# A gated DeltaNet layer on one core: TensorE's first stage in a written order of slots, and reciprocal square roots by GpSimd's power operation

## The chip, the cores and the metric

One core of a Trainium2 chip runs the whole kernel. The metric is the device time of one execution in microseconds (us), as the median of several executions. A profile is taken from one further execution. The engines are TensorE (PE; PEld is its weight load), VectorE (DVE), ScalarE (ACT), GpSimd (POOL) and SyncE (SP), whose queue issues all DMA transfers here.

## The reference

One layer of a streaming encoder, for 4096 prompt tokens and 32 sample tokens, with 1024 channels:

```python
h    = rmsnorm(x, ln_pre)
proj = h @ w_in            # B_a, C_a, X_a, Z_a | q, k, v | Z_g | a_dec, b_beta
y_a  = B_a * conv3(C_a * X_a) * silu(Z_a)                  # group A
q, k, v = silu(conv4(qkv));  q, k = l2norm(q), l2norm(k)   # group B, 4 heads of 128
S_t  = exp(g_t) (I - beta_t k_t k_t^T) S_{t-1} + beta_t k_t v_t^T
o_t  = q_t^T S_t / sqrt(128);  y_g = rmsnorm_head(o) * silu(Z_g)
y    = x + rmsnorm(concat(y_a, y_g) @ w_out, ln_post)
```

The recurrence is worked out in chunks. For a chunk, `a_mat` is the strictly lower part of `k k^T` with decay and beta, and `T = (I + a_mat)^-1`; with T the chunk's new values are a few matrix products with the state S, and S moves on to the next chunk.

## The kernel before

The prompt is cut into 16 blocks of 256 tokens (two chunks of 128), and the kernel has three stages. **Stage 1** (until about 1320 us) does group B, block by block. **Stage 2** does group A and **stage 3** the output projection. The change is in stage 1, and in the small function `rsqrt` that all stages call.

A block of stage 1 projects 16 channel tiles in pairs, in the order k, k, q, q, v, v, z, z (`steps`). One tile is 24 matmuls of 128x256 in fp16 (`proj`, L388 to L390: weights and activations are split in a high and a low half, 3 products for each of 8 slices). ScalarE and VectorE make the convolution and silu of each pair (`qkv_pair`). Beside that run, for the same block or the one before:

- `gates` and `decays`: decay and beta of the block's tokens (tiles `ggate`, `gcs`, `gB`).
- `stage1(b, c)`: for chunk c, 8 transposes (tile `gt`, L426) for the norms, and then 4 fp32 matmuls of 128x256 (tile `gq`, L442), from which VectorE writes M (L443: k k^T with decay) and `at`. Four DMAs bring M's diagonal 32x32 parts to DRAM (`lad`, L450).
- `subst(b)`, once for both chunks: DMAs load all 32 triangles into one tile `la` (L485); VectorE computes a scale `rl` (L488 to L490); GpSimd multiplies `la` by it (L495) and then solves the 32 triangular systems in 31 pairs of one multiply and one subtract (L499, L500), each resting on the one before; the result goes to DRAM (`ltd`, L503) and comes back in 8 DMAs as `Tc` (L510).
- `merge(b)`: from the inverses of the 32x32 parts in `Tc`, that of the whole 128x128 chunk (tile `m`, L546 to L560). It has five steps on TensorE, each after a copy of the one before. The first (below: M1) needs `Tc`.
- `rec_a(b, c)` and `rec_b(b, c)`: the recurrence and its output.
- `prep_a`: GpSimd, VectorE and 4 to 8 small matmuls prepare weights for stage 2 in the gaps of 13 of the blocks (tiles `xtw`, `hl`).

The main loop calls `finish(prevs, si)` for the block before: merge at step 0, then the recurrence; `stage1` stands at steps 4 and 5 of the block itself, one step earlier in the last two blocks (`LS`). That is the order in the code. The order on each engine's queue is decided by the Tile framework, which simulates the program and takes from each engine's ready instructions; it need not follow the code. An engine's queue runs strictly in the order so found.

`rsqrt(x, y, t)` is 11 small VectorE operations: an integer estimate and three Newton rounds (L114 to L119). It is called for the norms of x (`xss`, in `xprep`), of q and k (`r`, in `rnorms`), of each chunk's output (`so`, in `rec_b`: twice for a block), and in stage 3 (`oss`).

Of the kernel before, what the change touches and what calls it, by code (L numbers as in the profile page):

```python
# [10 lines left out]
BF16 = mybir.dt.bfloat16  # L11
# [23 lines left out]
LS = 2  # L35
# [15 lines left out]
def hybrid_kernel(  # L51
# [7 lines left out]
    V, G, A, T = nc.vector, nc.gpsimd, nc.scalar, nc.tensor  # L59
# [107 lines left out]

    def scaled(cts, n=P, urow=None):


        ws = []
        first = cts[0] >= 16
        nm = f"{cts[0]}"
        L = bank("r" if first else "g", [P, 2, P], f"L{nm}")[:, :len(cts), :n]
        for i, ct in enumerate(cts):
# [10 lines left out]
            if not first:  # L186
                for kn in (4, 2, 1):
                    V.tensor_tensor(ab[:, 0:kn], ab[:, 0:kn], ab[:, kn:2 * kn], ALU.add)
            for k in range(kn):
                T.matmul(L[:, i], ones16, ab[:, k, :], start=k == 0, stop=k == kn - 1)  # L190
            ws.append(w)
        e = te([P, 2, P], I32, "we", 1, nm)[:, :len(cts), :n]
# [8 lines left out]
        for i, w in enumerate(ws):  # L201
            V.tensor_tensor(w, w, bc(e[:, i].bitcast(F32), 1, KT), ALU.mult)
        if urow is None:
# [4 lines left out]
        return ws  # L208
# [13 lines left out]
    def xprep(b):  # L222
# [7 lines left out]
        ss = te([P, 3, 2], F32, "xss", 2, b["id"])[:m, :, :n // m]  # L230
# [12 lines left out]
        rsqrt(ss[:, 0], ss[:, 1], ss[:, 2])  # L243
# [138 lines left out]
    def proj(b, cts, nm):  # L382
        n = b["n"]
        pt = bank("pj", [P, 2, NB1], f"{b['id']}_{nm}")
        for i, ct in enumerate(cts):
            wh, wl = W[ct]
            for k in range(KT):
                T.matmul(pt[:, i, :n], wh[:, k, :], b["hi"][:, k, :n], start=k == 0, stop=False)  # L388
                T.matmul(pt[:, i, :n], wh[:, k, :], b["lo"][:, k, :n], start=False, stop=False)  # L389
                T.matmul(pt[:, i, :n], wl[:, k, :], b["hi"][:, k, :n], start=False, stop=k == KT - 1)  # L390
        return pt

    def qkv_pair(b, c0, dst):

        n = b["n"]
        pt = proj(b, (16 + c0, 17 + c0), f"c{c0}")
# [11 lines left out]
    def z_pair(b, c0):  # L408
        n = b["n"]
        pt = proj(b, (28 + c0, 29 + c0), f"z{c0}")  # L410
# [4 lines left out]
    def stage1(b, c):  # L415
# [4 lines left out]
        ss = b["ss"]  # L420
        nm = f"{b['id']}_{c}"
        jk = te([P, P], BF16, "jk", 2, nm)
        for x in range(2):
            tp = bank("g", [P, NH, P], f"t{x}{nm}")
            for h in range(NH):
                T.transpose(tp[:C, h, :], qk[:, h, x, sl], ident)  # L426
            for h in range(NH):
                A.activation(jk[:C], tp[:C, h, :], AF.Square, accum_out=ss[:, c, x, h:h + 1])
            if x == 0:
                kd = (te if b["s"] else tl)([P, NH, P], F32, "hl" if b["s"] else "kd", 4, nm)[:C]  # L430
                V.tensor_tensor(kd, tp[:C], bc(b["ed"][:, c], 2, P), ALU.mult)
                b["kd"].append(kd)
# [18 lines left out]

    def rnorms(b):
# [63 lines left out]
    def merge(b):  # L516
# [26 lines left out]
        for q in (0, 2):  # L543
# [3 lines left out]
            V.tensor_tensor(X[s1], px[s1], bc(nb_[s1], 3, 32), ALU.mult)  # L547
        for q in (0, 2):
# [16 lines left out]
    def rec_a(b, c):  # L565
# [4 lines left out]
        qk, v, U, kd = b["qk"], b["v"], b["U"][c], b["kd"][c]  # L570
        S = state[b["s"]]
# [21 lines left out]
        A.activation(vn, pv, AF.Copy)  # L593
        pS = bank("r", [P, NH, P], f"S{nm}")
# [6 lines left out]
        b["rec"] = (o, vn)  # L601

    def rec_b(b, c):
# [4 lines left out]
        o, vn = b["rec"]  # L608
# [4 lines left out]
        so = tl([P, 3, NH], F32, "so", 2, nm)[:C]  # L613
# [6 lines left out]
        rsqrt(so[:, 0], f, so[:, 2])  # L620
        V.tensor_tensor(f, f, b["cc"][:, c], ALU.mult)
        V.tensor_tensor(o, o, bc(f, 2, P), ALU.mult)
        pm = bank("o", [P, NH, P], f"m{nm}")[:, :, :C]
# [10 lines left out]
    def setup_block(b):  # L634
# [10 lines left out]
        b["kd"], b["M"], b["at"] = [], [], []  # L645

    def prep_b(ct):

        for i, w in enumerate(scaled((ct, ct + 1))):
# [6 lines left out]

    wa = {"next": 0}

    def prep_a():
# [7 lines left out]
        if not half:  # L667
            wa["w"] = scaled((ct, ct + 1))
# [70 lines left out]
    wgf, = scaled((32,), 8, ug)  # L739
# [8 lines left out]
    def finish(prevs, si):  # L748

        for p in prevs:  # L750
            n = p["nch"]
            if si == 0:
                merge(p)
            elif si == 1:
                rec_a(p, 0)
            elif si == 2:
                rec_b(p, 0)
                if n > 1:
                    rec_a(p, 1)
            elif si == 3:  # L760
                if n > 1:
                    rec_b(p, 1)
                if p["last"]:
                    out_state(p)

    prevs = []
    for gi, grp in enumerate(groups):
        for b in grp:
            setup_block(b)
            if b["s"]:  # L770
                b["hist"] = te([P, 12, 3], F32, "hists", 2, "i")
                if gi:
                    for c in range(0, 12, 2):
                        init_hist(b, 16 + c)
                state[1] = te([P, NH, P], F32, "hl", 4, "s0")
                dma(state[1], state_gdn[0, 0].rearrange("h k v -> k h v"))
            elif gi:
                b["hist"] = groups[gi - 1][-1]["hist_new"]
        for si, (kind, c0) in enumerate(steps):
            if gi == 0 and si == 4:  # L780
# [3 lines left out]
            if gi == 0:  # L784
                for kd_, c_ in steps[:si + 1 + (AH if si >= AS else 0)]:
                    ct = (28 if kd_ == "z" else 16) + c_
                    if ct not in W:
                        prep_b(ct)
                if kind != "z":
                    init_hist(smp, 16 + c0)  # L790
            for b in grp:
                n = b["n"]
                if kind == "z":
                    z_pair(b, c0)
                elif kind == "v":
                    qkv_pair(b, c0, b["v"][:, c0 - 8:c0 - 6, :n])
                else:
                    h0 = c0 % 4
# [454 lines left out]
```

## Time and profile before

| | |
|---|---|
| time, median of 3 (lowest to highest) | 2394.66 us (2390.61 to 2403.79) |
| the profiled execution: time, span | 2393.51 us, 2391.8 us |
| mean granted TensorE clock | 0.962 |
| busy: PE / PEld / DVE | 2156.4 / 1706.8 / 1699.0 us |
| busy: ACT / POOL | 992.5 / 1195.2 us |

The span runs from the first to the last instruction; the time is 1.7 us longer. PE is busy for 90% of the span, so it is near to being the bound as a whole. But a share over the whole span says nothing of one stage: in stage 1 a chain over all engines and four DMA legs runs beside the projections, and which of the two limits must be read from the waits there. The granted clock is the share of full speed that TensorE was allowed; 1 is 2.4 GHz, and 0.50 is 1.2 GHz.

### The profile page before, as it was taken

What the parts mean: (1) busy time and instruction counts of PE and PEld (TensorE: products, weight loads), DVE (VectorE), ACT (ScalarE), POOL (GpSimd) and SP (SyncE); (2) the same over time, 40 slices, a digit from 0 to 9 for tenths busy, and PEclk for the clock granted to TensorE, in tenths of its full rate; (3) what the DMA queues carried; (4) which work ended last, traced back from release to release, by engine and by line L of the source; (5) the groups of instructions that cost most, each with busy time, mean ns of one, the idle gap of its engine ahead of it and who ended that gap; (6) DMA issues with size and microseconds to landing.
All of it is one profiled execution on the core that took longest, in us unless ns stands there. A gap on an engine that the chain in (4) does not pass through costs nothing. (4 is left out here: it accounts for less than half of the span.)

```text
span 2391.8 us, 48652 instructions
## 1 busy us (share of the span) xinstructions
PE 2156.4 (90%) x18626; PEld 1706.8 (71%) x18626; DVE 1699.0 (71%) x4666; ACT 992.5 (41%) x2497; POOL 1195.2 (50%) x1581
## 2 busy tenths in 40 slices
PE   3677989899999999999999799899999999999998
PEld 3566877778777777787778678788888887444443
DVE  4886878987689888786777675676575565666763
ACT  4454656565666566555654220222121121433321
POOL 3526246752575644454454740766456611554542
PEclk9888999999999999999989899999999999999999
DMA  6334333534333442244324304311211133443431
GB/s 117 53 93 106 80 75 96 116 82 92 92 100 78 109 112 75 68 91 118 70 72 125 101 24 174 104 66 54 80 59 39 54 100 98 136 150 115 157 115 54
DMA packets 296913, 221.39 MB, mean 93 GB/s; under 512 B 166392, under 2 KB 236856, under 8 KB 296680
## 3 DMA queue, kind: packets, MB, share of 16 engines
q1 hardware_dynamic: 296680, 218.28, 33.5%
q8 instruction: 146, 2.39, 0.4%
q14 instruction: 87, 0.71, 0.1%
HBM read 127.84 MB, written 74.64 MB: 85 GB/s over the span
## 5 line engine op out<-in xcount | busy, mean ns | idle before, releaser
L388 PE MATMUL pj_c<-hhi,w 128*128 128x256 f16 x1536 | 429.3, 280 | 1.2 <-DMA hhi<-xth 1.2
L390 PE MATMUL pj_c<-hhi,w 128*128 128x256 f16 x1536 | 429.7, 280 | 0.0
L389 PE MATMUL pj_c<-hlo,w 128*128 128x256 f16 x1536 | 428.9, 279 | 0.0
L867 PEld LDWEIGHTS <-w_a 128*128 128x128 f16 x2880 | 269.9, 99 | 59.5 <-issue 25.6
L1130 PEld LDWEIGHTS <-opm 128*128 128x128 f16 x1536 | 149.6, 98 | 189.8 <-issue 15.5
L500 POOL TENSOR_TENSOR lt<-lt 128x112 f32<-128x112 f32 (+29 forms) x496 | 250.0, 504 | 38.9
L495 POOL TENSOR_TENSOR la<-la,lt 128x1024 f32<-128x1024 f32 x16 | 38.7, 2421 | 449.9 <-DVE lt L490 270.9
L390 PEld LDWEIGHTS <-w 128*128 128x128 f16 x2176 | 215.5, 100 | 53.2 <-POOL w L652 23.0
L499 POOL TENSOR_TENSOR lt<-la,lt 128x112 f32<-128x112 f32 (+29 forms) x496 | 233.1, 470 | 38.8
L388 PEld LDWEIGHTS <-w 128*128 128x128 f16 x2176 | 215.8, 100 | 34.1 <-issue 2.1
L389 PEld LDWEIGHTS <-w 128*128 128x128 f16 x2176 | 215.7, 100 | 30.7 <-issue 0.5
L405 DVE SCALAR_TENSOR_TENSOR qk<-u,cw,qk 128x256 f32<-128x256 f32 x384 | 214.9, 596 | 9.0 <-ACT qk L403 8.4
L867 PE MATMUL pja<-op,w_a 128*128 128x256 f16 x1536 | 194.5, 276 | 7.0 <-DVE w L881 3.4
L1079 POOL TENSOR_TENSOR mab<-mab 128x1024 bf16<-128x1024 bf16 (+2 forms) x48 | 103.6, 2159 | 130.8 <-ACT mab L1077 128.4
L867 PE MATMUL ga<-op,w_a 128*128 128x256 f16 x1152 | 149.8, 275 | 14.0 <-DVE w L881 8.1
L389 PE MATMUL pj_z<-hlo,w 128*128 128x256 f16 x512 | 144.6, 282 | 0.0
L390 PE MATMUL pj_z<-hhi,w 128*128 128x256 f16 x512 | 144.4, 282 | 0.0
L388 PE MATMUL pj_z<-hhi,w 128*128 128x256 f16 x512 | 144.3, 282 | 0.0
L1130 PE MATMUL pjo<-w_o,opm 128*128 128x512 f16 x528 | 118.2, 379 | 3.8 <-DVE v13y L1154 2.0
L1130 PE MATMUL ro<-w_o,opm 128*128 128x512 f16 x504 | 114.7, 383 | 3.9 <-DVE v7y L1154 2.0
L881 DVE TENSOR_TENSOR w<-pja,w 128x256 f32<-128x256 f32 x168 | 67.4, 420 | 70.6 <-PE pja L867 68.0
L1130 PE MATMUL go<-w_o,opm 128*128 128x512 f16 x504 | 112.7, 379 | 3.9 <-DVE v19y L1154 2.0
(707 smaller groups left out, 4946.5 us busy)
## 6 DMA issues: line engine op xcount, KB each, us to landing
xt<-in_x_prompt_dram SPq DMA_DIRECT2D x32, 512.0 KB
op<-hTd SPq DMA_DIRECT2D x32, 512.0 KB
mx<-mxd SPq DMA_DIRECT2D x16, 1024.0 KB
xtw<-in_w_in_dram SPq DMA_DIRECT2D x28, 512.0 KB
wad<-hl SPq DMA_DIRECT2D x56, 256.0 KB
gB<-gd SPq DMA_DIRECT2D x16, 516.0 KB
hTd<-hhi SPq DMA_DIRECT2D x16, 512.0 KB
hTd<-hlo SPq DMA_DIRECT2D x16, 512.0 KB
```

Of the source, the lines that this page charges most:

```text
L388: T.matmul(pt[:, i, :n], wh[:, k, :], b["hi"][:, k, :n], start=k == 0, stop=False)
L389: T.matmul(pt[:, i, :n], wh[:, k, :], b["lo"][:, k, :n], start=False, stop=False)
L390: T.matmul(pt[:, i, :n], wl[:, k, :], b["hi"][:, k, :n], start=False, stop=k == KT - 1)
L405: V.scalar_tensor_tensor(d, u[:, i, j:j + n], cw[:, j, c0 + i:c0 + i + 1], d, ALU.mult, ALU.add)
L495: E.tensor_tensor(la, la, bc(rl, 1, 32), ALU.mult)
L499: E.tensor_tensor(tm, bc(la[:, j, j + 1:32], 2, w), bc(lt[:, j, 0:w], 1, r), ALU.mult)
L500: last = E.tensor_tensor(lt[:, j + 1:32, 0:w], lt[:, j + 1:32, 0:w], tm, ALU.subtract)
L867: T.matmul(out, lt(x, k), rh(y, k), start=start and k == n == 0, stop=stop and k == 3 and n == 2)
L881: V.tensor_tensor(dst, p, src, ALU.add)
L1079: G.tensor_tensor(ab[:, 0:m], ab[:, 0:m], ab[:, m:2 * m], ALU.add)
L1130: T.matmul(p, mo[:, x, k, t * P:t * P + m], WO[y, k][:, hf * 512:hf * 512 + 512], start=k == i == 0, stop=k == KT - 1 and i == 2)
```

## The change

Four things, of which the diff shows the core:

1. Every TensorE instruction goes through a small class `Ordered`. While `T.on` is true (from block 1 to the end of stage 1) each is chained behind the one before, so that PE's queue is exactly the order of the code.
2. The code of blocks 1 to 15 is written in slots. A block has 16 slots, one after each channel tile, and a function cut into parts by `yield` runs its parts in numbered slots. M1 of block g stands in slot 8 of block g+1 (`s0 + 24`), the other merge steps in slots 9 to 12, the two `gram` (the `gq` matmuls and M) in slots 11 and 12, the transposes for the norms of k in 7 and 8 and of q in 10 and 11, `gates` in 9, 10 and 13. Blocks of stage 1 no longer differ at the end (`LS` is gone).
3. `rsqrt(x, y)` is one GpSimd operation, `pow` with an operand of -0.5.
4. `prep_a` is called after channel tile 7, waits for the previous block's `subst_end` alone, and its matmuls (now 2 instead of 8, after one more VectorE addition) stand in slots 11 and 13.

```diff
+    class Ordered:
+        on = False
+        last = None
+        def queue(self, i):
+            ins = getattr(i, "ins", i)
+            if self.on and self.last is not None:
+                tc.add_manual_dep(ins, self.last.name, mybir.DependencyInfo(
+                    mybir.DependencyClass.NoSync, mybir.DependencyReason.DATA), reason="order")
+            self.last = ins
+            return i
...
-    def rsqrt(x, y, t):
-
-        V.tensor_scalar(t.bitcast(I32), x.bitcast(I32), 1, None, ALU.logical_shift_right)
-        V.tensor_scalar(y.bitcast(I32), t.bitcast(I32), -1, float(0x5F3759DF), ALU.mult, ALU.add)
-        for _ in range(3):
-            V.tensor_tensor(t, y, y, ALU.mult)
-            V.scalar_tensor_tensor(t, t, -0.5, x, ALU.mult, ALU.mult)
-            V.scalar_tensor_tensor(y, t, 1.5, y, ALU.add, ALU.mult)
+    mhalf = const([P, 16], F32, "mhalf")
+    V.memset(mhalf, -0.5)
+
+    def rsqrt(x, y):
+
+        G.tensor_tensor(y, x, mhalf[:x.shape[0], :x.shape[-1]], ALU.pow)
...
+    def finish(p, s0):
...
+        at_slot(s0 + 22, next, ra[0])
+        at_slot(s0 + 23, next, ra[0])
+        for i in range(5):
+            at_slot(s0 + 24 + i, next, mg, None)
+        at_slot(s0 + 29, next, ra[0])
+        at_slot(s0 + 30, ends, ra[0])
+        at_slot(s0 + 30, next, rb[0])
+        at_slot(s0 + 28, next, ra[1])
+        at_slot(s0 + 32, next, ra[1])
+        at_slot(s0 + 34, next, ra[1])
+        at_slot(s0 + 34, ends, rb[0])
+        at_slot(s0 + 35, ends, ra[1])
+        at_slot(s0 + 35, next, rb[1])
+        at_slot(s0 + 39, ends, rb[1])
...
-            s1 = 4 if gi + LS < len(groups) else 3
-            if si in (s1, s1 + 1):
...
+            at_slot(s0 + 7, norm_qk, b, 0, 0)
+            at_slot(s0 + 8, norm_qk, b, 1, 0)
+            at_slot(s0 + 10, norm_qk, b, 0, 1)
+            at_slot(s0 + 11, gram, b, 0)
+            at_slot(s0 + 11, norm_qk, b, 1, 1)
+            at_slot(s0 + 12, gram, b, 1)
+            at_slot(s0 + 12, rnorms, b)
+            at_slot(s0 + 12, subst, b)
+            if gi + 1 < len(groups):
+                nx = groups[gi + 1][0]
+                g = gates(nx)
+                at_slot(s0 + 2, xprep, nx)
+                at_slot(s0 + 9, next, g)
+                at_slot(s0 + 10, next, g)
+                at_slot(s0 + 13, ends, g)
+            finish(b, s0)
+            for si, (kind, c0) in enumerate(steps):
+                ps = pair(b, kind, c0)
+                next(ps)
+                run_slot(s0 + 2 * si)
+                ends(ps)
+                run_slot(s0 + 2 * si + 1)
```

What it moves on the engines, at three places.

On TensorE before, M1 of one block (tile `m`, from `Tc` and `M`) stands inside a z tile (`w_30`) of the next one, a matmul at a time, and the `gq` of that next block begins between them:

```order
L388 MATMUL pj_z_15005<-hhi_13353,w_30_1926 128x256
L546 MATMUL m_14092<-Tc_13862,M_0_13648 32x32
L389 LDWEIGHTS w_30_1926
L389 MATMUL pj_z_15005<-hlo_13354,w_30_1926 128x256
L546 MATMUL m_14092<-Tc_13862,M_0_13648 32x32
L442 MATMUL gq_0_14702<-qk_14019 128x256 x2
L546 MATMUL m_14092<-Tc_13862,M_0_13648 32x32
L390 LDWEIGHTS w_30_1927
L390 MATMUL pj_z_15005<-hhi_13353,w_30_1927 128x256
```

M1 and the next block's `gq` stand side by side there, in the fifteenth of the block's 16 channel tiles.

On TensorE after, M1 is one piece behind the ninth tile (`w_24`, slot 8):

```order
L74 MATMUL pj_c_16834<-hhi_15618,w_24_1191 128x256
L74 MATMUL m_16864<-Tc_16303,M_0_16129 32x32 x4
L74 MATMUL m_16864<-Tc_16303,M_1_16199 32x32 x4
L74 MATMUL m_16864<-Tc_16303,M_0_16129 32x32 x4
L74 MATMUL m_16864<-Tc_16303,M_1_16199 32x32 x4
L77 MATMUL gt_1_16884<-ident,qk_16473 128x128 x4
L74 LDWEIGHTS w_25_1194
L74 MATMUL pj_c_16834<-hhi_15618,w_25_1194 128x256
```

It moved from the fifteenth tile to behind the ninth, and needs all 8 parts of `Tc` at once, where before the first needed one.

Further on in the same block, the second `gram` behind the thirteenth tile (`w_28`, slot 12):

```order
L74 MATMUL pj_z_17066<-hhi_15618,w_28_1487 128x256
L74 MATMUL m_16864<-U,Rx_16863 64x64 x8
L77 MATMUL rt_1_17100<-ident,v_15493 128x128 x4
L74 MATMUL gq_1_17112<-qk_16473 128x256 x2
L74 MATMUL gq_1_17117<-qk_16473 128x256 x2
L74 LDWEIGHTS w_29_1490
```

All of the merge and four channel tiles now stand between M1 and the `gq` of the next block.

On GpSimd before, `subst` runs through without anything between (`hl` in front is a weight of `prep_a`):

```order
L675 TENSOR_TENSOR hl_6_7578<-xtw_6500,hl_6_7578 128x512
L495 TENSOR_TENSOR la_8463<-la_8463,lt_8464 128x1024
L499 TENSOR_TENSOR lt_8464<-la_8463,lt_8464 128x31
L500 TENSOR_TENSOR lt_8464<-lt_8464 128x31
L499 TENSOR_TENSOR lt_8464<-la_8463,lt_8464 128x60
```

And after (L137 is the power operation; a third one, of the other chunk's `so`, stands further down among the pairs):

```order
L137 TENSOR_TENSOR r_13209<-ss_12458,mhalf 128x16
L544 TENSOR_TENSOR la_13218<-la_13218,lt_13219 128x1024
L548 TENSOR_TENSOR lt_13219<-la_13218,lt_13219 128x31
...
L548 TENSOR_TENSOR lt_13219<-la_13218,lt_13219 128x112
L137 TENSOR_TENSOR so_0_13417<-so_0_13417,mhalf 128x4
L549 TENSOR_TENSOR lt_13219<-lt_13219 128x28x4
L548 TENSOR_TENSOR lt_13219<-la_13218,lt_13219 128x135
L549 TENSOR_TENSOR lt_13219<-lt_13219 128x27x5
L548 TENSOR_TENSOR lt_13219<-la_13218,lt_13219 128x156
L137 TENSOR_TENSOR xss_13595<-xss_13595,mhalf 128x2
```

The powers came into GpSimd's queue in front of and inside the chain of the solve.

## Rows read from the trace of the kernel before

**Rows 1.** Busy times over twelve blocks: all engines; then PE on `m`, `gq`, `gt`, `ggate`.
```profile
core 0: us, PE busy (x) PEld busy (x) DVE busy (x) ACT busy (x) POOL busy (x), PEclk, DMA share, GB/s
331.20:1248.60 917.40, 850.74 (x7949) 721.04 (x7947) 744.12 (x2272) 535.60 (x1434) 501.89 (x904) 0.96 0.38 92
331.20:1248.60 917.40, 86.96 (x1286) 0.96 0.38 92
331.20:1248.60 917.40, 53.23 (x192) 0.96 0.38 92
331.20:1248.60 917.40, 33.76 (x192) 0.96 0.38 92
331.20:1248.60 917.40, 12.51 (x384) 0.96 0.38 92
```

**Rows 2.** Waits of PE, 200 to 1370 us: total us, times, longest.
```profile
PE m L546 <- DMA Tc<-ltd: 25.4, 17, 3.0
```

**Rows 3.** VectorE's timeline (start us, us) and summary of M, L443.
```profile
269.50 0.42 DVE L443 TENSOR_TENSOR M<-gq,gB 128x256 f32<-128x256 f32 x1
566.49 0.42 DVE L443 TENSOR_TENSOR M<-gq,gB 128x256 f32<-128x256 f32 x1
858.76 0.42 DVE L443 TENSOR_TENSOR M<-gq,gB 128x256 f32<-128x256 f32 x1
1173.67 0.42 DVE L443 TENSOR_TENSOR M<-gq,gB 128x256 f32<-128x256 f32 x1
L443 DVE TENSOR_TENSOR M<-gq,gB x64: 404/424/426, 161.7 to 1310.2; 128x256 f32<-128x256 f32 x64
```

**Rows 4.** PE's timeline: two projections, M1 of three blocks.
```profile
619.37 0.27 PE L388 MATMUL pj_z<-hhi,w 128*128 128x256 f16 x1
619.48 0.27 PE L389 MATMUL pj_z<-hlo,w 128*128 128x256 f16 x1
622.38 0.24 PE L546 MATMUL m<-Tc,M 32*32 32x32 f32 x2 [2.41 <-DMA Tc<-ltd]
630.33 0.69 PE L546 MATMUL m<-Tc,M 32*32 32x32 f32 x16
1370.91 0.31 PE L546 MATMUL m<-Tc,M 32*32 32x32 f32 x2 [6.09 <-DMA Tc<-ltd]
```

**Rows 5.** GpSimd's timeline: first and last operations of `subst` in three blocks.
```profile
580.92 2.48 POOL L495 TENSOR_TENSOR la<-la,lt 128x1024 f32<-128x1024 f32 x1 [46.28 <-DVE lt L490]
868.69 2.36 POOL L495 TENSOR_TENSOR la<-la,lt 128x1024 f32<-128x1024 f32 x1 [23.74 <-DVE xss L115]
907.34 0.20 POOL L500 TENSOR_TENSOR lt<-lt 128x8 f32<-128x8 f32 x1
1187.60 2.47 POOL L495 TENSOR_TENSOR la<-la,lt 128x1024 f32<-128x1024 f32 x1 [27.57 <-DVE lt L490]
1221.02 0.20 POOL L500 TENSOR_TENSOR lt<-lt 128x8 f32<-128x8 f32 x1
```

**Rows 6.** VectorE's timeline: the first and the last `rl` of one block.
```profile
575.91 0.19 DVE L488 TENSOR_SCALAR lt<-la 128x32 f32<-128x32 f32 x1
580.60 0.19 DVE L490 TENSOR_TENSOR lt<-lt,bl 128x32 f32<-128x32 f32 x1
```

**Rows 7.** SyncE's timeline: the way back of one block's solve.
```profile
618.67 0.34 SPq L503 DMA_DIRECT2D ltd<-lt  x1
620.39 4.29 SPq L510 DMA_DIRECT2D Tc<-ltd  x8
```

**Rows 8.** GpSimd's operations by shape: busy us, mean ns; then idle before.
```profile
L499 POOL TENSOR_TENSOR lt<-la,lt 128x16 f32<-128x16 f32 x16 | 4.3, 271 | 1.3
```

**Rows 9.** Two stretches around PE's longest gap (columns as in rows 1).
```profile
226.00:233.70 7.70, 0.42 (x5) 0.13 (x3) 3.57 (x9) 2.35 (x9) 5.58 (x20) 0.70 0.04 2
233.70:239.00 5.30, 5.30 (x25) 3.99 (x26) 0.00 (x0) 1.47 (x8) 0.74 (x5) 0.50 0.37 42
```

**Rows 10.** Summary of a line of `rsqrt`: duration ns min/median/max.
```profile
L117 DVE TENSOR_TENSOR so<-so x96: 99/163/1109, 292.6 to 1436.7; 128x4 f32<-128x4 f32 x96
```

More of the change, by code (lines that the diff above doesn't have):

```diff
@@ L34 @@
 SG = 0
-LS = 2
 XPE = 256
@@ L186, in scaled @@
             if not first:
-                for kn in (4, 2, 1):
-                    V.tensor_tensor(ab[:, 0:kn], ab[:, 0:kn], ab[:, kn:2 * kn], ALU.add)
-            for k in range(kn):
+                ab2 = e[:, i, 0:P // 2].bitcast(BF16)
+                for kn, o in ((4, ab[:, 0:4]), (2, ab[:, 0:2]), (1, ab2.unsqueeze(1))):
+                    V.tensor_tensor(o, ab[:, 0:kn], ab[:, kn:2 * kn], ALU.add)
+                sums.append(ab2)
+            for k in range(kn if first else 0):
                 T.matmul(L[:, i], ones16, ab[:, k, :], start=k == 0, stop=k == kn - 1)
             ws.append(w)
-        e = te([P, 2, P], I32, "we", 1, nm)[:, :len(cts), :n]
+        if not first:
+            yield
+            L = bank("g", [P, 2, P], f"L{nm}")
+            for i in range(2):
+                T.matmul(L[:, i], ones16, sums[i], start=True, stop=True)
         V.tensor_scalar(e.bitcast(F32), L, 2.0 ** -100, None, ALU.max)
@@ L202, in scaled @@
             V.tensor_tensor(w, w, bc(e[:, i].bitcast(F32), 1, KT), ALU.mult)
+        if not first:
+            yield
         if urow is None:
@@ L450, in stage1 @@
             dma(b["lad"][c, :, q].rearrange("h j i -> j h i"), M[s, :, s])
+    def stage1(b, c):
+        norm_qk(b, c, 0)
+        norm_qk(b, c, 1)
+        gram(b, c)
     def rnorms(b):
@@ L555, in merge @@
         A.activation(Y[0:64], pt, AF.Copy)
+        yield
         for c, h in ch:
@@ L667, in prep_a @@
         if not half:
-            wa["w"] = scaled((ct, ct + 1))
+            yield from scaled((ct, ct + 1))
             return
@@ L746, in hybrid_kernel, with at_slot, run_slot, ends @@
     steps = [("k", 4), ("k", 6), ("q", 0), ("q", 2), ("v", 8), ("v", 10), ("z", 0), ("z", 2)]
[L748 to L767, printed above, removed]
+    slots = {}
+    def at_slot(i, fn, *a):
+        slots.setdefault(i, []).append(lambda: fn(*a))
+    def run_slot(i):
+        for fn in slots.pop(i, ()):
+            fn()
+    def ends(gen):
+        for _ in gen:
+            pass
+    def finish(p, s0):
+        n = p["nch"]
+        ra = [rec_a(p, c) for c in range(n)]
+        rb = [rec_b(p, c) for c in range(n)]
+        mg = merge(p)
+        if n == 1:
+            for i, g in enumerate((ra[0], ra[0], mg, ra[0], ra[0], rb[0])):
+                at_slot(s0 + 16 + i, next, g, None)
+            at_slot(s0 + 24, ends, rb[0])
+            at_slot(s0 + 24, out_state, p)
+            return
+        at_slot(s0 + 22, next, ra[0])
[12 more added lines that the diff above has]
+        at_slot(s0 + 39, ends, rb[1])
+        if p["last"]:
+            at_slot(s0 + 36, out_state, p)
+    def first_group(grp):
         for b in grp:
@@ L826, in hybrid_kernel @@
         prevs = grp
-    while wa["next"] < 16:
-        prep_a()
+    T.on = False
     early.close()
-    for si in range(4):
-        finish(prevs, si)
+    for i in sorted(slots):
+        run_slot(i)
     late.close()
```

190 lines of the change are left out of this document (109 added, 81 removed).

## The prediction

> **What bounds the kernel now.** The page gives PE 90% of the span, so I first looked at whether stage 1 is bound by PE's work or by something that PE waits for. Over twelve blocks PE is busy for 850.74 of 917.40 us [rows 1]: 70.9 us of work for a block, and 5.6 us of idle time. The times at which a block's M is written come every 75.35 us: (1173.67 + 0.42 - 269.50 - 0.42) / 12 [rows 3]. So PE is close to the bound, and not quite there.
>
> The waits of PE then show what it is idle for: most of all `Tc`, 25.4 us in 17 waits, 3.0 at the longest [rows 2]. So there is a second bound that lies just as close, and it is a loop. A block's M goes through the DMAs and GpSimd's solve and comes back as `Tc` (I call this the chain); with `Tc` PE does M1 and some more work up to the next block's `gq`, from which the next M is written (the PE part). The period can't be shorter than chain plus PE part, whatever is in PE's queue elsewhere.
>
> The chain is read part by part, each from the rows of one block:
> - From M to GpSimd's first multiply: 858.76 + 0.42 to 868.69, which is 9.5 us; in another block 566.49 + 0.42 to 580.92, which is 14.0 [rows 3, 5]. In the latter the three small `rl` operations lay 4.7 us apart, 575.91 to 580.60, with other VectorE work between them [rows 6].
> - The solve: 1187.60 to 1221.02 + 0.20 is 33.6 us, 868.69 to 907.34 + 0.20 is 38.9 [rows 5].
> - The way back: `ltd` is issued at 618.67, the first `Tc` at 620.39, the eighth 4.29 us later [rows 7]; M1's first matmul ran at 622.38 [rows 4], 2.0 us behind the first issue. It needed the first part alone.
>
> So the chain to the first matmul of M1 lasts about 9.5 + 33.6 + 3.7 = 46.8 to 14.0 + 38.9 + 3.7 = 56.6 us, and with 75.35 as period some 19 to 28 us are left for the PE part. That part is short because M1 and `gq` stand side by side in PE's queue.
>
> **The change part by part.**
>
> *The slots.* After the change M1 stands behind tile 8 and the last `gq` behind tile 12. The PE part becomes a fixed list:
> - four channel tiles, 4 x 24 matmuls at 0.11 us (619.37 to 619.48, [rows 4]): 10.6
> - the merge: 8 of its 56 matmuls in one piece took 0.69 us [rows 4], which gives 4.8; in the loop as it is they take 86.96 / 12 = 7.2 [rows 1]. I take 5.5, nearer to the former, since they stand in pieces now.
> - both `gq`: 53.23 / 12 = 4.4; three quarters of the transposes `gt`: 33.76 / 12 x 3/4 = 2.1; `ggate`: 12.51 / 12 = 1.0 [rows 1]; the four transposes `rt` like `gt`: 4 x 0.176 = 0.7
> - M behind the last `gq`: 0.6, one operation of 0.42 [rows 3] and the way to it.
>
> That is 24.9 us. The chain now ends with the eighth `Tc`, since M1 is one piece: 1.7 us to the first issue, 4.3 for all eight, some 1.5 to land, 7.5 in all [rows 4, 7]. For its head I take 9.5, because VectorE gets relief (below) and the `rl` stand together; 14.0 is the other end. For the solve I take the middle, 36.2.
>
> PE has work for 70.9 - 24.9 = 46 us between the last `gq` and M1. The chain, worked out next, takes longer than that, so PE will stand before M1 in every block, with the z, k and q tiles that could fill the time locked behind it in the queue.
>
> *The powers.* One `rsqrt` on VectorE was 11 operations of about 0.163 us [rows 10], so 1.8 us; four in a block give back 7.2 us of VectorE. VectorE is busy for 744.12 of 917.40 us [rows 1], it isn't the bound, and the relief is worth only what it brings to the chain's head. On GpSimd, one power (`r`) lies ahead of the first multiply, in time in which GpSimd waits for `la` anyway; three stand inside the solve, and the solve is the path. No row shows a power. The lower bound is a multiply of nearly its size, 0.27 us for 128x16 [rows 8]; the upper one the multiply of 128x1024, 2.4 us [rows 5]. I take 0.8, between them in ratio, because it is a costlier function on a tiny tile: 3 x 0.8 = 2.4 us on the path. Their inputs come from the block before and the next `xprep`; if one is late, the solve waits for it.
>
> The Trainium skill, GPSIMD Engine Reference, section "4.1 Engine selection", speaks against the move: elementwise work on a tile belongs to VectorE, and GpSimd is about 2 times slower with two inputs. By that a power would be an estimated 2 x 0.163 = 0.33 us, and the sum 14 x 3 x 0.47 = 20 us lower, 2479; no row here shows a power.
>
> *The clock.* The only gap as long as the one I expect is at 226.00 to 233.70, where PE worked for 0.42 us; behind it PE ran for 5.30 us at a granted clock of 0.50, the level of 1.2 GHz [rows 9]. That loses 2.65 us, in the PE part, each time. The durations I used hold the mean clock 0.96 [rows 1], which is 1.0 us of 24.9; so 1.7 more.
>
> The Trainium skill, TensorE: Matmul & The Clock Gate, section "HAM oscillation — how this bites in real kernels", describes just that, bursts of matmuls between waits for data that each start at the lower clock. The row agrees; without the effect the sum would be 14 x 1.7 = 24 us lower, 2475.
>
> *The rest.* Chaining PE's instructions costs no time by itself, they ran in order already. `prep_a` gives up 6 small matmuls and takes a VectorE addition, off the path. The end of the last two blocks, where `LS` moved the `gram` forward, loses that: these two periods took 1310.2 + 0.42 - 1174.09 = 136.5 us together [rows 3].
>
> **The sum.** Chain 9.5 + 36.2 + 2.4 + 7.5 = 55.6. Period 55.6 + 24.9 + 1.7 = 82.2 us. Twelve periods: 12 x (82.2 - 75.35) = +82. The last two: 164.4 - 136.5 = +28. I leave the first block and stages 2 and 3 as they are, less the 6.09 us for which PE stood at the last M1 [rows 4], of which I take 5 back. In all +105 us on the profiled execution's 2393.51, which is 1.15 below the median: **2499 us**.
>
> **The rivals.**
> - *The chain at its shortest.* Solve 33.6, powers at 0.27, no loss of clock: 9.5 + 33.6 + 0.8 + 7.5 + 24.9 = 76.3. Then 12 x 0.95 + (152.6 - 136.5) - 5 = +22, 2416 us. For it: VectorE and GpSimd disturb each other less. Against: the long solve of 38.9 is as well attested as the short one.
> - *`Tc` comes before slot 8* (other side). If the chain falls below 70.9 - 24.9 = 46 us, PE never waits and the period is PE's work, 70.9: 12 x -4.45 + (141.8 - 136.5) - 5 = -53, 2340 us. The kernel becomes faster at all if the period falls below (12 x 75.35 + 136.5 + 5) / 14 = 74.7, so a chain under 49.8. For it: the VectorE relief, and PE's 5.6 us of idle time in small waits that a fixed order may remove. Against: the shortest parts that any of these rows shows, with the cheapest power, make 51.4.
> - *Dear powers.* At 2.4 us each, or with waits for their inputs that stop the solve for as long: 3 x 1.6 = 4.8 more a period, 14 x 4.8 = +67, 2566 us. For it: nothing else in these rows has as many inputs that come from elsewhere in the middle of the solve. Against: the tiles have 2 and 4 columns.
>
> **How the numbers follow.** The loop as summed 0.60, with a range of its own of 2435 to 2565 (the head at 9.5 to 14.0, the solve at 33.6 to 38.9, the merge at 4.8 to 7.2, not all at one end); the short chain 0.14; dear powers 0.12; `Tc` in time 0.14. The predicted time is the first's. From 2400 to 2580 all but the last case and the ends of the others lie inside, about 0.8. A measurement of this kernel can't tell less than 0.5%, 12 us, from no change. The fourth case gives faster 0.12 and 0.02 near no change; the second 0.04 near no change; all else is slower, 0.82.
>
> **What would show it.** Right: a wait of PE for `Tc` at M1 of about 10 us in each of 14 blocks, with the clock at 0.50 behind it; M every 82 us; M1 to the next M 25 to 28 us; chain 53 to 58 us; L137 rows on GpSimd under 1 us. Wrong: no wait at M1 (the fourth case), M every 76 us or less, power rows of 2 us, or a solve with gaps ahead of its powers. It would also be wrong if the solve itself became much shorter once VectorE does less beside it: that is the one large term that I carry over from before without a reason of its own.

## The result and the profile after

The changed kernel takes 2571.06 us (2564.86 to 2576.26, 4 runs) against 2394.26 us: a ratio of 1.073, with a 95% interval of 1.069 to 1.077. The profiled execution took 2564.86 us, 171 us more than that of before; the sums below are made against it.

The page's busy line and its row of TensorE's granted clock in 40 slices:

```profile
PE 2202.4 (86%) x18626; PEld 1755.8 (69%) x18626; DVE 1526.9 (60%) x3732; ACT 1003.2 (39%) x2497; POOL 1303.6 (51%) x1666
PEclk9878988888898889889988988999999999999999
```

VectorE lost 172 us of work and GpSimd gained 108. PE is busy for 46 us more, partly because its clock is lower. So most of the time went into waiting; the lower clocks are in the first 24 of the 40 slices, which are stage 1. M's rows on VectorE give the period, as in [rows 3]:

```profile
273.31 0.42 DVE L488 TENSOR_TENSOR M<-gq,gB 128x256 f32<-128x256 f32 x1
1334.99 0.42 DVE L488 TENSOR_TENSOR M<-gq,gB 128x256 f32<-128x256 f32 x1
L488 DVE TENSOR_TENSOR M<-gq,gB x64: 414/424/426, 160.8 to 1500.3; 128x256 f32<-128x256 f32 x64
```

Twelve periods took 1061.7 us, 88.5 each, against 75.35. The 171 us are made up of +3.8 up to the first of these rows, 12 x 13.1 = +157.5, +28.8 in the last two periods (1500.72 - 1335.41 = 165.3, before 136.5), and -18.8 from the last M to the end (2563.1 - 1500.7, before 2391.8 - 1310.6).

Over twelve blocks (columns as in [rows 1]), and what PE waited for there (as in [rows 2]):

```profile
369.50:1431.30 1061.80, 882.72 (x7905) 759.41 (x7903) 633.93 (x1725) 543.22 (x1436) 541.24 (x942) 0.89 0.33 77
```

```profile
PE m L74 <- DMA Tc<-ltd: 81.6, 108, 6.5
PE om L77 <- DVE o L679: 37.7, 7, 12.4
PE oo L74 <- DVE zg L685: 32.8, 13, 3.5
PE m L74 <- DVE Rx L596: 29.8, 14, 2.3
```

PE is idle for 14.9 us of a block (1061.80 - 882.72, over 12) and not 5.6, and the mean clock fell from 0.96 to 0.89. The largest wait is the one forecast, for `Tc` at M1: 81.6 us over the 14 blocks of this window, 5.8 a block, where the prediction expected about 10. Three others, at `om`, `oo` and in M1's second half, were not in the sum.

One M1 on PE's timeline shows both kinds. The eight parts of `Tc` come 0.55 us apart; then the second half waits for VectorE's product of the first:

```profile
1301.23 0.31 PE L74 MATMUL m<-Tc,M 32*32 32x32 f32 x2 [3.63 <-DMA Tc<-ltd]
1301.83 0.31 PE L74 MATMUL m<-Tc,M 32*32 32x32 f32 x2 [0.29 <-DMA Tc<-ltd]
...
1305.11 0.31 PE L74 MATMUL m<-Tc,M 32*32 32x32 f32 x2 [0.23 <-DMA Tc<-ltd]
1307.44 1.05 PE L74 MATMUL m<-Tc,M 32*32 32x32 f32 x16 [2.01 <-DVE Rx L596]
```

The clock in this block, ahead of M1, in it, and from there to the next M:

```profile
1250.90:1299.70 48.80, 44.40 (x388) 39.73 (x385) 32.90 (x80) 26.46 (x70) 35.42 (x68) 0.97 0.43 104
1299.70:1313.40 13.70, 8.46 (x56) 6.08 (x57) 3.28 (x7) 3.88 (x12) 11.19 (x15) 0.51 0.45 119
1313.40:1335.40 22.00, 21.14 (x216) 17.31 (x215) 11.59 (x46) 14.33 (x37) 2.91 (x1) 0.92 0.06 16
```

GpSimd's powers by shape, and two of one solve on its timeline:

```profile
L137 POOL TENSOR_TENSOR r<-ss,mhalf 128x16 f32<-128x16 f32 x16 | 46.6, 2913 | 353.4 <-DVE ss L507 353.4
L137 POOL TENSOR_TENSOR so<-so,mhalf 128x4 f32<-128x4 f32 x32 | 32.5, 1016 | 60.0 <-DVE so L676 30.2 <-DVE hist L429 27.3 <-ACT o L642 1.2
L137 POOL TENSOR_TENSOR xss<-xss,mhalf 128x2 f32<-128x2 f32 x16 | 11.2, 701 | 10.4 <-DVE xss L271 10.4
```

```profile
462.97 1.01 POOL L137 TENSOR_TENSOR so<-so,mhalf 128x4 f32<-128x4 f32 x1 [0.83 <-DVE so L676]
500.26 1.01 POOL L137 TENSOR_TENSOR so<-so,mhalf 128x4 f32<-128x4 f32 x1 [12.40 <-DVE hist L429]
```

The three powers inside the solve take 2 x 1.02 + 0.70 = 2.7 us. The second one of this solve held it up for 12.4 us more, since its input was not there. That is the longest such wait: GpSimd's idle time ahead of its powers is 0.8 to 13.2 us in each of the twelve solves of the table below, 4.2 in the mean.

The input was late because of `prep_a`, the fourth part of the change. VectorE makes the input (`so`, L676), and ahead of it in VectorE's queue stood the first operation on a weight of `prep_a`, which waited for the DMA of that weight:

```profile
497.74 1.23 DVE L204 TENSOR_TENSOR xtw<-xtw,lnp 128x1024 f32<-128x1024 f32 x1 [10.17 <-DMA xtw<-in_w_in_dram]
499.95 0.16 DVE L676 TENSOR_SCALAR so<-so 128x4 f32<-128x4 f32 x1
```

In the kernel before, the same operation never waited. Its group in stage 1, before and after; behind the second bar is VectorE's idle time ahead of it:

```profile
L182 DVE TENSOR_TENSOR xtw<-xtw,lnp 128x1024 f32<-128x1024 f32 x16 | 19.0, 1218 | 0.0
L204 DVE TENSOR_TENSOR xtw<-xtw,lnp 128x1024 f32<-128x1024 f32 x14 | 18.4, 1316 | 54.2 <-DMA xtw<-in_w_in_dram 54.2
```

In seven of the twelve solves the second power waits behind such a stop, for 37.0 of the 49.9 us that all powers wait there. PE's seven waits at `om` follow these seven stops, each some 5 us later.

### The profile page after: what moved, and what is told of

The parts are those of the page before. It is cut to its first block, busy times and chain, and to the rows that moved or that the text cites. A ratio compares the mean times of both kernels' runs of the same rounds, so it can differ in the third digit from the quotient of the medians.

```text
span 2563.1 us, 47756 instructions
## 1 busy us (share of the span) xinstructions
PE 2202.4 (86%) x18626; PEld 1755.8 (69%) x18626; DVE 1526.9 (60%) x3732; ACT 1003.2 (39%) x2497; POOL 1303.6 (51%) x1666
## 5 line engine op out<-in xcount | busy, mean ns | idle before, releaser
L74 PE MATMUL pj_c<-hhi,w 128*128 128x256 f16 x3072 | 590.6, 292 | 2.2 <-ACT u L428 2.2
L74 PE MATMUL pj_c<-hlo,w 128*128 128x256 f16 x1536 | 449.0, 292 | 0.0
L549 POOL TENSOR_TENSOR lt<-lt 128x112 f32<-128x112 f32 (+29 forms) x496 | 241.7, 487 | 37.1
L548 POOL TENSOR_TENSOR lt<-la,lt 128x112 f32<-128x112 f32 (+29 forms) x496 | 220.9, 445 | 37.1
L137 POOL TENSOR_TENSOR r<-ss,mhalf 128x16 f32<-128x16 f32 x16 | 46.6, 2913 | 353.4 <-DVE ss L507 353.4
L74 PE MATMUL pj_z<-hhi,w 128*128 128x256 f16 x1024 | 179.1, 273 | 0.9 <-ACT u L428 0.9
L74 PE MATMUL m<-Tc,M 32*32 32x32 f32 x512 | 54.0, 236 | 118.9 <-DMA Tc<-ltd 87.1
L74 PEld LDWEIGHTS m<-Tc,M 32*32 32x32 f32 x512 | 35.8, 138 | 141.2 <-DMA Tc<-ltd 104.3
L466 ACT ACTIVATE jk<-gt 128x128 bf16<-128x128 f32 x256 | 71.0, 278 | 138.7 <-PE gt L77 132.8
L1000 ACT ACTIVATE op<-tsc 128x512 f16<-128x512 f32 x60 | 37.7, 629 | 185.6 <-POOL tsc L1006 108.9
```

The costliest lines, as they stand in the source:

```text
L74: return self.queue(nc.tensor.matmul(*a, **k))
L137: G.tensor_tensor(y, x, mhalf[:x.shape[0], :x.shape[-1]], ALU.pow)
L466: A.activation(jk[:C], tp[:C, h, :], AF.Square, accum_out=b["ss"][:, c, x, h:h + 1])
L548: E.tensor_tensor(tm, bc(la[:, j, j + 1:32], 2, w), bc(lt[:, j, 0:w], 1, r), ALU.mult)
L549: last = E.tensor_tensor(lt[:, j + 1:32, 0:w], lt[:, j + 1:32, 0:w], tm, ALU.subtract)
L1000: A.activation(f[:, q, 0, hf], t, AF.Copy)
```

## The experiments

Each ran with the kernel before on the same chip, 4 or more runs; the kernel before took 2394 to 2398 us each time. The table sets them side by side. The four columns on the right are means over the twelve periods behind the second M, worked out from the rows of M (VectorE), of the first `la` multiply and the last subtract (GpSimd) and of M1's first matmul (PE) in each trace.

| run | time, us | ratio to before (95%) | period | solve | M to M1 | M1 to next M |
|---|---|---|---|---|---|---|
| before | 2394.3 | | 75.4 | 37.3 | 54.2 | 21.1 |
| changed | 2571.1 | 1.069 to 1.077 | 88.5 | 42.6 | 54.8 | 33.7 |
| 1 slots, VectorE's rsqrt | 2542.6 | 1.059 to 1.068 | 85.9 | 35.2 | 55.8 | 30.1 |
| 2 powers alone | 2389.8 | 0.996 to 1.000 | 75.9 | 39.0 | 55.2 | 20.7 |
| 3 two slots later | 2520.3 | 1.049 to 1.057 | 86.6 | 41.7 | 62.9 | 23.7 |
| 4 waits filled | 2616.4 | 1.088 to 1.098 | 90.2 | 42.6 | 56.4 | 33.8 |
| 5 queue not chained | 2433.4 | 1.012 to 1.018 | 80.1 | 42.2 | 55.2 | 24.9 |
| 6 M1 in one piece | 2531.8 | 1.053 to 1.058 | 86.7 | 43.0 | 55.4 | 31.3 |
| 7 more slots | 2526.1 | 1.051 to 1.056 | 86.2 | 42.4 | 54.8 | 31.4 |
| 8 more slots, VectorE's rsqrt | 2513.5 | 1.045 to 1.051 | 84.9 | 35.7 | 54.7 | 30.2 |
| 9 more slots, short solve | 2463.2 | 1.026 to 1.031 | 82.2 | 31.6 | 50.1 | 32.1 |
| 10 more slots, two later | 2481.1 | 1.033 to 1.038 | 84.1 | 38.1 | 59.3 | 24.8 |
| 11 before, long solve | 2429.6 | 1.012 to 1.016 | 78.2 | 40.8 | 58.1 | 20.0 |
| 12 before, powers but two | 2420.4 | 1.009 to 1.012 | 79.4 | 37.8 | 55.8 | 23.6 |

**1. Slots with VectorE's rsqrt.** The function and its calls are those of before:

```diff
-        G.tensor_tensor(y, x, mhalf[:x.shape[0], :x.shape[-1]], ALU.pow)
+        V.tensor_scalar(t.bitcast(I32), x.bitcast(I32), 1, None, ALU.logical_shift_right)
...
```

> The changed kernel with its slots, but every rsqrt again as 11 VectorE operations. Theory (the loop of chain and PE part sets the period, and the powers are one term of the chain): the solve loses the 2.7 us of three powers and about 3.7 us of waits in front of them, 6.4 a block; the head of the chain, 8.3 us now, grows back by 1 to 3 us since VectorE is busier. Net 3.4 to 5.4 us x 14 blocks: about 2571 - 60 = 2510 (2495 to 2525). Rival (the powers are what makes the change slow): near or below the kernel before, under 2430. Rival (the powers and their waits lie beside other waits of PE): 2560 or more.

Only 28 us came back, between the theory and the rival that the powers lie beside other waits. The solve did get 7.4 us shorter. But M1 hardly waited for `Tc` any more (8.8 of the 16.6 us below are in one block, the last but one), and the time went to other stops; the 52.1 us at `om` stand again in the seven blocks in which VectorE stops for a weight of `prep_a`. In its waits:

```profile
PE om L77 <- DVE o L682: 52.1, 7, 17.3
PE oo L74 <- DVE zg L688: 45.1, 13, 4.8
PE m L74 <- DVE Rx L599: 32.3, 14, 4.3
PE m L74 <- DMA Tc<-ltd: 16.6, 18, 7.9
```

**2. The powers alone**, in the kernel before:

```diff
-        V.tensor_scalar(t.bitcast(I32), x.bitcast(I32), 1, None, ALU.logical_shift_right)
...
+        G.tensor_tensor(y, x, mhalf[:x.shape[0], :x.shape[-1]], ALU.pow)
```

> The kernel before with its order left to the framework, and every rsqrt as one GpSimd power. Theory: the chain gains 2.7 us of powers in the solve, and loses 2 to 3.7 us at its head from VectorE's relief: nearly nothing, 2380 to 2425. Rival (powers and the waits for their inputs cost the 6 us a block that the solve grew by in the changed kernel): 2394 + 14 x 6 = about 2480. Rival (VectorE's relief is worth more than the powers cost): under 2370.

No change that can be measured, as the theory has it: 1.7 us more in the solve, less ahead of it. What the powers do to the changed kernel, they do through the place that they got in its queues.

**3. Two slots later.** M1 in slot 10, and all that follows it:

```diff
-        at_slot(s0 + 22, next, ra[0])
-        at_slot(s0 + 23, next, ra[0])
+        at_slot(s0 + 24, next, ra[0])
+        at_slot(s0 + 25, next, ra[0])
         for i in range(5):
-            at_slot(s0 + 24 + i, next, mg, None)
+            at_slot(s0 + 26 + i, next, mg, None)
...
```

> The changed kernel with all of finish (merge and recurrence of the block before) two slots later, M1 in slot 10 and not 8; gram stays in slots 11 and 12. Theory: two channel tiles leave the PE part for the chain's side, 5.3 us at full clock and more at half clock, and the wait for Tc (4 us and its clock loss behind it) becomes small: period 88.5 - 7 to 11, so 2571 - 14 x 9 = about 2445 (2415 to 2475). Rival (the many local waits that any fixed order brings make the period, not the loop): within 1% of 2571.

51 us less, 75 short of the theory. The PE part fell by 10 us as expected, and the wait for `Tc` is gone from the list, but PE took 8 us longer to come to M1. Other waits had grown:

```profile
PE m L74 <- DVE Rx L596: 73.3, 14, 7.5
PE rS L74 <- ACT vn L649: 40.5, 16, 4.4
PE om L77 <- DVE o L679: 27.7, 4, 8.1
PE oo L74 <- DVE zg L685: 20.9, 4, 10.0
```

From here on the theory has two bounds: the loop, and the pace of a chained queue with all its stops, which lies only a few us below it.

**4. Waits filled** with matmuls that nobody needs:

```diff
+        wd = W[20][0].rearrange("p k c -> p (k c)")
         for q in (0, 2):
+            for _ in range((48, 20)[q // 2]):
+                T.matmul(pm[:, 256:512], wd[:, 0:P], wd[:, 0:256], start=True, stop=True)
```

> The changed kernel with 48 extra fp16 matmuls of 128x256 (5.2 us) ahead of M1 and 20 (2.2 us) between its halves, into a part of PSUM that is overwritten later, so that PE has work while Tc comes. Nothing else is changed, and the outputs are the same. Theory, with the clock as the term that the prediction had too small: of 17 us at half clock behind the wait for Tc in a block most run at full clock, 5 to 7 us less a block: 2571 - 14 x 6 = about 2487 (2470 to 2510). Rival (the wait itself counts and not the clock behind it, as the prediction had it): the extra work only fills the wait, or delays M1 by up to 3 us: 2560 to 2610.

45 us slower, just above the rival's range. It tells little of the clock, because the second filling did not fill: the 20 matmuls waited for the same product as M1's second half, and ran at 0.52 behind it, 4.43 us instead of 2.2, on the path. They are not what made the run slower, though: from M1 to the next M it took 33.8 us, as long as without them, so PE's other work there took that much less. Of the 1.7 us that a period grew by, 1.6 lie ahead of M1, and 17 us of the 43 between the two profiled executions lie behind the last M; the runs don't show why.

```profile
1317.19 5.40 PE L74 MATMUL m<-w 128*128 128x256 f16 x48
1322.52 0.60 PE L74 MATMUL m<-Tc,M 32*32 32x32 f32 x8
...
1327.92 4.43 PE L74 MATMUL m<-w 128*128 128x256 f16 x20 [2.01 <-DVE Rx L599]
```

**5. The queue not chained**; slots, code order and powers stay:

```diff
-            T.on = True
```

> The changed kernel with its slots and powers, but PE's instructions are not chained: the framework orders PE's queue again, from code that stands in the new order. Theory (the chained queue is the cause: PE stops at each step whose input is late, and has other work standing behind it): within 1.5% of the kernel before, 2360 to 2430. Rival (the new order of the code, the place of gram and prep_a, and the powers are the cause, whoever orders the queue): 2500 or more.

138 of the 177 us are gone, just above the theory's 2430. So the chaining is the cause of most. The code's new order and the powers keep a period of 80.1, and leave 1.5%.

The table shows where the chain costs it: M to M1 is as long as in the changed kernel (55.2 against 54.8), and M1 to the next M falls from 33.7 to 24.9. About the same projections stand there, 98 matmuls of 128x256 in the mean and not 102, but PE is idle for 0.1 us of it and not 5.1. One such part of the changed kernel, then one of this run (columns as in [rows 1]):

```profile
1301.23:1335.42 34.19, 29.62 (x270) 23.41 (x271) 14.89 (x53) 18.21 (x49) 12.57 (x13) 0.77 0.19 52
```

```profile
1193.96:1217.77 23.81, 23.65 (x228) 18.71 (x229) 15.48 (x49) 14.47 (x36) 11.13 (x13) 0.86 0.27 75
```

In the kernel before this part took 21.1 us. So of the 12.6 us that the change adds to it, about 3.8 come with the new order of the code, and 8.8 with the fixed queue: its stops (5.0), and 3.7 in which PE is busy longer, at a lower clock and with some more small matmuls of the merge.

**6. M1 in one piece**, and the second merge step likewise:

```diff
             for c, h in ch:
                 T.matmul(px[s1, c, h], M[c][s0, h, s1], Tc[s0, c, h], start=True, stop=True)
+        for q in (0, 2):
+            s1 = slice(32 * q + 32, 32 * q + 64)
             V.tensor_tensor(X[s1], px[s1], bc(nb_[s1], 3, 32), ALU.mult)
```

> The changed kernel with all 16 matmuls of M1 ahead of the two VectorE products, and all 16 of the second merge step ahead of the two ScalarE copies: the second half of M1 waits 2.1 us for the first product now, that of the second step 0.5. Theory (every stop of the chained queue counts, with the half clock behind it): 2.5 to 5 us a block, 2571 - 50 = 2520 (2495 to 2540). Rival (the wait moves on to the second step, whose input comes as late as before): 2560 or more.

39 us, as the theory has it: 2.4 us less from M1 to the next M.

**7. More slots for the recurrence**, with 6:

```diff
-        at_slot(s0 + 30, ends, ra[0])
-        at_slot(s0 + 30, next, rb[0])
+        at_slot(s0 + 31, ends, ra[0])
+        at_slot(s0 + 31, next, rb[0])
...
-        at_slot(s0 + 35, next, rb[1])
-        at_slot(s0 + 39, ends, rb[1])
+        at_slot(s0 + 38, next, rb[1])
+        at_slot(s0 + 42, ends, rb[1])
```

> As the run with M1's matmuls first, and besides the steps of the recurrence that stand one slot behind the step whose result they take get two or three: PE stops there for 2.4 us (oo, for the one bank that om still holds), 0.7 to 2 us (rS, for vn) and 3 us in the mean (om, for o). M1 and gram keep their slots. Theory (all stops of the chained queue count): another 3 to 5 us a block, 2571 - 14 x 7 = about 2470 (2440 to 2500). Rival (only the loop from M over the solve to M1 and the next gram counts, and the recurrence lies beside it): as the run with M1's matmuls first, within 15 us.

Here the rival was right: 6 us less than run 6, within its 15. The stops at `oo` and `om` went away, and PE waited longer for `Tc` (88.7 us in all, 85.4 in run 6). With the loop binding, what lies beside it is nearly free. In a block without delays this run shows the loop in full: M at 1226.46 + 0.42, M1 at 1278.04, M at 1307.40 + 0.42, which is 51.2 + 29.8 = 80.9 us.

```profile
1226.46 0.42 DVE L488 TENSOR_TENSOR M<-gq,gB 128x256 f32<-128x256 f32 x1
1307.40 0.42 DVE L488 TENSOR_TENSOR M<-gq,gB 128x256 f32<-128x256 f32 x1
```

```profile
1278.04 0.31 PE L74 MATMUL m<-Tc,M 32*32 32x32 f32 x2 [6.42 <-DMA Tc<-ltd]
```

**8. More slots, VectorE's rsqrt**: the edits of 1 and 7 together.

> The run with more slots for the recurrence and with rsqrt as 11 VectorE operations again. In the run with slots and VectorE's rsqrt M1 hardly waits for Tc any more (0 in most blocks), and PE stops at M1's second half for 2 to 4 us, at oo for 3 to 4.6, at rS for 1 to 2.3 and at om for 2 to 17. Theory (all stops count): 2543 - 14 x 7 to 9 = about 2430 (2400 to 2460). Rival (the loop alone): 2543 - 14 x 2.5 = about 2508 or more.

2513: 83 us above the theory's figure and at the loop rival's 2508 or more; but the loop does not bind here (M1 waits for `Tc` for 5.1 us in all blocks up to 1450 us together). Without the powers the solve was 6.7 us shorter, and PE's stops kept most of it: 67.6 us at `om`, 38.4 at M1's product, 21.5 at `rv` for R.

**9. More slots, short solve**: 7 of 31 pairs are not computed.

```diff
-        for j in range(31):
+        for j in [x for x in range(31) if x % 4 != 3 or b["s"]]:
```

> The run with more slots for the recurrence, and every fourth of the solve's 31 pairs left out (7 pairs of the prompt's blocks; that part of the triangular solve is not computed), so that the chain gets 8 to 9 us shorter and nothing else changes. Theory (the loop from M over the solve to M1 and the next gram sets the period in that run, 51 us of chain and 30 of PE part in the blocks without delays): the period falls by as much as PE waits at M1 now, 1.3 to 6.4 us a block and 1.7 between its matmuls, then PE's own pace holds it: 2526 - 14 x 4.5 = about 2460 (2440 to 2485). Rival (the stops of PE's queue set the period, of which the wait for Tc is one that another would replace): 2510 or more.

63 us less than run 7, as the theory has it: the loop was the bound there. But 10.8 us came off the solve and 4.0 off the period. Now PE's pace is the bound, with other names in its list:

```profile
PE m L74 <- DVE Rx L598: 45.2, 11, 7.9
PE rq L74 <- ACT R L633: 18.2, 13, 2.9
PE oo L74 <- DVE zg L689: 14.9, 4, 5.3
PE m L74 <- DMA Tc<-ltd: 10.9, 36, 0.4
```

**10. More slots, two later**: the edits of 3 and 7 together.

> The run with more slots for the recurrence, with all of merge and recurrence two slots later: M1 in slot 10, gram in 11 and 12. Theory (two bounds that lie close together, the loop and the stops of PE's queue; here both are eased): two channel tiles less in the PE part, 5.3 us, of which some 4 are seen: 2526 - 14 x 4 = about 2470 (2445 to 2490). Rival (as in the run with two slots alone, other stops take the place of the wait for Tc): 2510 or more.

45 us less, as the theory has it. The list of stops is new again: `gt` for a free bank (37.5 and 18.5 us), `om` (32.5), M1's product (17.9).

**11. A long solve in the kernel before**: 6 of its multiplies are done twice.

```diff
+            for _ in range(2 if 7 <= j < 13 and not b["s"] else 1):
                 E.tensor_tensor(tm, bc(la[:, j, j + 1:32], 2, w), bc(lt[:, j, 0:w], 1, r), ALU.mult)
```

> The kernel before, with 6 of the solve's 31 multiplies done twice (same result), 0.75 to 0.85 us each with what lies between: the chain gets 4.5 to 5 us longer, on an engine that is busy for half of the time. Theory (before the change too the loop sets the period, as the prediction has it): 2395 + 14 x 3.5 to 5 = about 2455 (2440 to 2470). Rival (before the change PE's work sets the period, and the loop has room): under 2415.

35 us, between the two. M to M1 got 3.9 us longer and the period 2.8: in the main the loop was the bound in the kernel before too. The other 1.1 us came off between M1 and the next M, in an order that the framework made anew.

**12. The kernel before with all powers but those of the recurrence's output:**

```diff
-        rsqrt(so[:, 0], f)
+        rsqrt_v(so[:, 0], f, so[:, 2])
```

> The kernel before, with order left to the framework; the rsqrt of q and k, of x and of stage 3 as GpSimd powers, and that of the recurrence's output, whose two powers lie inside the solve with the waits for their inputs, by VectorE as before. Theory (the loop): VectorE's relief stays for the most part and the solve gets its 2 us and the waits back, against the run with all powers 2 to 3 us a block: 2390 - 14 x 2.5 = about 2355 (2340 to 2375), faster than both kernels. Rival (what VectorE has to do for the output is in the loop as well): 2385 to 2400.

Wrong: 2420, slower than the kernel before and than run 2. The solve fell by 1.2 us against run 2, but the way from M to it grew from 11.5 to 13.6 us in the mean, in some blocks to over 22: the framework's new order put the transfers of M behind others on SP's queue. So this run doesn't price the two powers.

No run beats the kernel before by what can be measured; run 2 comes nearest.

## Why the prediction was right, and where it fell short

The direction, the loop as its mechanism and the place of the wait were right. It gave 105 us of the 171; the period was to be 82.2 and was 88.5. The totals make the miss look smaller than it is: 6.3 us a period and 3.8 ahead of the first, against 13.8 that stage 3 gave back beyond the forecast. Point by point:

- **Two near bounds before the change.** Run 11 bears out the loop. That PE's work lies close under it was read from [rows 1], and no run tests it.
- **M1 and `gq` side by side.** "That part is short because M1 and `gq` stand side by side in PE's queue" is not so in most blocks of the kernel before; the order shown ahead of the prediction is that of one block. In the twelve blocks of the table M1's first matmul to the next M took 4.8 to 31.6 us, with 1 to 137 projection matmuls in between, 82 in the mean. In the longest:

```profile
991.64 0.24 PE L546 MATMUL m<-Tc,M 32*32 32x32 f32 x2 [1.75 <-DMA Tc<-ltd]
1022.81 0.42 DVE L443 TENSOR_TENSOR M<-gq,gB 128x256 f32<-128x256 f32 x1
```

After the change it is 102 in every block. So the slots put less than one channel tile (24 matmuls) more into this part, in the mean, and not four; most of what it grew by is the price of the fixed queue (run 5). The forecast's sum stands without this reading, since it counts the list as it is after.
- **M to M1.** In the prediction's parts this was 9.5 + 36.2 + 2.4 + 3.7 = 51.8 us to the first matmul; it measured 54.8. The head was near (8.4 us, with the `rl` together), and so was the price of a power (2.7 us for three against 2.4). The step that failed: "if one is late, the solve waits for it" stood there at a price of nothing. The solve took 42.6 us and not 38.6, with 4.2 us of waits ahead of its powers, and 35.2 without powers (run 1). Behind three quarters of these waits is a second step that failed: `prep_a` "takes a VectorE addition, off the path". Its stops on VectorE hold up the input of a power, and so the path. No run moved `prep_a` alone, so what its place costs in all stays open. Two of the prediction's own signs of being wrong are there, "a solve with gaps ahead of its powers" and "power rows of 2 us" (the 128x16 power ahead of the solve takes 2.9). By the Trainium skill's rule (GPSIMD Engine Reference, "4.1 Engine selection"), whose row is of adds, multiplies and maxima, a power was to cost an estimated 0.33 us; the rows have 1.02 for 128x4, and the measurement decides.
- **M1 to the next M.** 3.8 + 24.9 + 1.7 = 30.4 us in the prediction, 33.7 measured. The list of work was right: with M1 in one piece and room for the rest, the clean block of run 7 has 29.8. What was missing is the stop inside M1, 2.0 us, a smaller one in the second step, and the half clock around them. Run 6 takes out 2.4 us of it.
- **The clock.** 2.65 us were to be lost at half clock. In the block shown PE was busy for 8.46 us at 0.51 and for 21.14 at 0.92: 4.1 + 1.7 = 5.8 us. The trace agrees with the rule cited from the Trainium skill (TensorE: Matmul & The Clock Gate, "HAM oscillation — how this bites in real kernels"): behind the 3.63 us for which PE stood before M1 the granted clock was 0.51. How much of these 5.8 us lies on the path was not separated; run 4 was to do that and did not. Run 5 gives a limit to what the fixed queue adds by it: 3.7 us of busy time.
- **The last blocks.** +28 forecast, +28.8 measured, in part by luck: the two periods were 85.4 and 79.9 us. The last one was shorter, among other things, because its solve (36.7 us) had two powers in it and waited for them only 1.1 us, which the forecast did not have.
- **Stage 3.** "I leave stages 2 and 3 as they are, less 5" was too small; 18.8 us came back. In 200 us of stage 3 that answer to each other, PE before and after:

```profile
2110.60:2310.60 200.00, 190.23 (x886) 0.99 0.38 127
```

```profile
2300.70:2500.70 200.00, 200.00 (x943) 1.00 0.42 140
```

There a power takes 11 VectorE operations out of PE's way, for 10 us in this stretch; in run 1, without powers, PE is busy for 189.88 of 200 us there. That is the part of the change that gains, and in run 2 it pays for the powers' cost in stage 1: up to the last M that run is 9.4 us longer than the kernel before, and from there on 15.4 shorter. Powers in stage 3 alone were not tried.

- **The rival "`Tc` in time"** was wrong in its price. It had PE run at its work, 70.9 us a block, once the loop lets go. Runs 1, 3, 8, 9 and 10 let the loop go, and the period stayed at 82 to 87. A chained queue has a pace of its own: where a step stands one slot (2.6 us) behind the step whose result it takes, over VectorE or ScalarE, PE stopped with projections behind it that run 5 puts into the gap. In run 9 the chain was 8.5 + 31.6 + 7.5 = 47.6 us (the last term is the prediction's), under the 49.8 from which the change was to be a gain, and the kernel was still 2.8% slower than before.
- **The rival "Dear powers"**, with 2566 us, lies nearest to what was measured, in part by luck. Its second form is what happened, waits that stop the solve: it took 4.0 us longer than forecast, and the rival had 4.8. But it lacks the 3.3 us a period from M1 to the next M, and hits the time because the head was shorter and stage 3 gave more back.
- **"Chaining PE's instructions costs no time by itself"** is the sentence that run 5 contradicts, if it is read beyond the loop: with the same code and powers, the chain alone is worth 138 us.

## What to carry to other kernels

Before fixing an engine's order by hand, find the loop that goes through it and place its two ends (here M1 and `gram`) close together: all that stands between them is paid in every turn. Then give each other step as many slots behind its input as the way over the other engines takes, by the profile, since a fixed queue has nothing to fill a late step with (with run 6's edit that gave 29 us from run 1 to 8 and 39 from run 3 to 10). Here no chained variant came down to the order that the framework makes of the changed kernel's code, 2433 us. Follow the inputs of each step back through the other queues too: a load that is late for work off the path can stand in front of work that is on it. Shortening the chain helps only down to the next bound; price that one, with its stops, before counting on the gain. And an operation that is cheap in itself is dear in a queue where the critical work stands behind it and its own input may be late.

## What the hardware showed that was not expected

A power on GpSimd grows with its columns on 128 partitions: 0.70 us for 2, 1.02 for 4, 2.91 for 16, about 0.16 a column. In stage 3 the same operation on 128x2 took 3.26 us in the mean of 15: 3.90 in twelve of them, and 0.71 in the other three. All twelve run beside eight VectorE operations with two inputs and end 0.6 us behind the last; the three have none of these beside them:

```profile
L137 POOL TENSOR_TENSOR oss<-oss,mhalf 128x2 f32<-128x2 f32 x15 | 48.9, 3261 | 104.8 <-DVE oss L1252 104.8
```

```profile
2226.27 0.71 POOL L137 TENSOR_TENSOR oss<-oss,mhalf 128x2 f32<-128x2 f32 x1 [7.48 <-DVE oss L1252]
2257.30 3.90 POOL L137 TENSOR_TENSOR oss<-oss,mhalf 128x2 f32<-128x2 f32 x1 [8.35 <-DVE oss L1252]
2257.39 3.24 DVE L1199 SCALAR_TENSOR_TENSOR mx<-mx,rm,msc 128x256 f32<-128x256 f32 x8
```

So the power seems to wait until VectorE is through with them; no run takes the two apart.
